# Two conditioning products moved from the second attention into the first feed-forward

## The chip, the core and the metric

The kernel runs on one core of a Trainium2 chip. A core has five engines that run their own instruction streams and meet at semaphores: TensorE (PE, with its weight loads shown as PEld), VectorE (DVE), ScalarE (ACT), GpSimd (POOL) and SyncE (SP). SP issues nearly all transfers here, one after the other from one queue; the transfers themselves are carried by the core's 16 DMA engines. The metric is the device time of one execution in microseconds (us); less is better. The times below are medians over runs, and the profile is of one further execution.

## The reference

One inference step of a two-layer encoder for 1024 prompt positions and 8 x 16 sample positions (1152 tokens, width 1024). Both layers have the same frame; `c` is a conditioning vector, one for the prompt and one for each sample:

```
ada = silu(c) @ w_ada[l] + b_ada[l]        # six pieces of 1024: shift, scale, gate, twice
h   = x * (1 + sc_m) + sh_m
x   = layer_norm(ALPHA * x + (1 + g_m) * attention(h))
h   = x * (1 + sc_f) + sh_f
x   = layer_norm(ALPHA * x + (1 + g_f) * conv_ffn(h))
```

The first layer attends over its own chunk of 64 and the two before it, the second over its own and the eight before it, with keys and values that are projected once from the first layer's output under a shift and scale of their own. `conv_ffn` projects up to 2 x 2816 columns, applies a causal convolution of width 3, multiplies `gelu` of one half by the other, and projects down. Sample positions have caches of keys, values and convolution rows.

## The kernel before

Everything is in 32 bit. A product of activations and weights is made of three passes over a high and a low part of each (`mmT`, L266, and `mmX`, L278); ACT makes the high part of a weight tile and POOL or DVE the low part (`split`, L160), after SP has loaded it into one of the two staging buffers `ws` (`wload`, L164). The parts go into a ring of weight slots.

The stages follow each other: first attention, its output projection, first feed-forward, second attention, its output projection, second feed-forward.

**The conditioning products.** The conditioning is 7 x 2048 columns, in seven products that `ada(gi, bank, ring)` computes: 0, 1 and 2 are the first layer's, 3 is that of the shared keys and values, 4, 5 and 6 are the second layer's. One product takes 16 loads of 512 KB of `in_adaw` (L207) and two float32 matmuls for each (L210) into one PSUM bank, with only 32 columns of `c` as the stationary side. Then it loads its bias four times (L197), adds it (L222), for products 1, 2, 5 and 6 adds 1 to the gate's part on POOL (L229) and writes that to `gd` in DRAM (L230), and brings the rest into `adaT` by four transposes (L235) and a copy (L237). A product is a generator: it yields after each load with its two matmuls, and after each part of its end, 18 steps in all.

Products run in the background of other work: `self.bg` holds a list of them, and `step(n)` adds `n` to a sum and runs one step of the list for each whole 1 in it. In the feed-forward `wload` calls it once for each weight tile, with `self.bgrate`; in the attention the loop over pairs calls it once a pair with `BGA` (0.6). `drain()` runs what is left. The buffers of a product are those of its ring: without one, the two `ws` buffers; in the first feed-forward `fr`, three buffers of `F` (`hf`, `xr`, `tmp`) that lie idle there until its last group.

**The attention** (`attention(l)`) first projects keys and values and writes them to DRAM (`kH` with a high and a low part, `vH` with both). Its loop then runs over 16 heads with four pairs of query blocks each. A head's keys are loaded by `kload` (L433), once a head for the high part and once for the low part, into buffers of which there is one set for even and one for odd heads:

```
for t, k in ((khi[a], kh), (klo[a], kl)):
    nc.sync.dma_start(t.bitcast(F32), bass.AP(k.tensor, k.offset, [[0, 2], [1024, 64], [1, 1024]]))
```

For each pair PE makes scores (L504, L507), DVE and ACT the softmax (L470, L474), PE transposes the weights (L530) and multiplies them by the values (L549). Query projections (L266, weights through `ws`) and 16 sample items with loads of their caches (L597 to L605; products at L615 and L650) are spread through the loop. Scores rotate over four PSUM banks; the products of the background use a bank of their own, bank 4, and once the list is empty scores rotate over five.

**The feed-forward** (`ffn(l)`) goes through 22 tile columns in groups of two: up-projections (L266), convolution on ACT and DVE (L978, L981), and the down-projection of the group before (L1052). The order in which each engine gets its instructions is made by a scheduler from the program, before the kernel runs; on the chip every engine keeps to it.

Of the kernel before, what the change touches and what calls it, by code (L numbers as in the profile page):

```python
# [32 lines left out]
UP = ({0: (0, 1), 2: (2,)}, {0: (0, 1), 3: (2,)})  # L33
LV = (0, 1, 2, 8, 3, 4, 5, 6, 7)
BGA = 0.6
BGF = 0.8
QAT = {}
for c in range(5):
    QAT[8 * c] = [(c + 1, None)]
# [48 lines left out]
class Trunk:  # L88
# [1090 lines left out]
    def build(self):  # L1179
        nc, I, O = self.nc, self.I, self.O  # L1180
        self.bgrate = 0
        ct = self.F[:, 12288:12544]
        nc.sync.dma_start(ct, I["cT"])
        nc.sync.dma_start(self.lnT, I["lnT"])
        nc.scalar.activation(self.cT, ct, AF.Exp, scale=-1.0)
        nc.vector.tensor_scalar_add(self.cT, self.cT, 1.0)
        nc.vector.reciprocal(self.cT, self.cT)
        nc.vector.tensor_mul(self.cT, self.cT, ct)
        x1 = self.x1p.tile([128, 9216], F32, name="x1in", tag="x1")
        big = [self.F[:, i * 1024 : i * 1024 + 1024] for i in range(10)]  # L1190
        big = Ring(big + [x1[:, i * 1024 : i * 1024 + 1024] for i in range(3, 9)])
        xs = [t.rearrange("p (c t) -> p c t", t=384) for t in (x1[:, 0:3072], self.F[:, 0:3072], self.F[:, 3072:6144])]
        for _ in self.ada(0, 0, big, self.F[:, 10240:11264]):
            pass
        wk = [self.wload(I["wk0"][0], el="v")]
        nc.sync.dma_start(xs[0], I["xT"][0])
        wk.append(self.wload(I["wk0"][1]))
        self.first_h(self.affine(0, (0, 1), e="v"), xs)
        self.bg = [self.ada(1, 4), self.ada(2, 4)]
        self.tables()  # L1200
        self.attention(0, wk)
        self.drain()
        aff = self.affine(0, (3, 4), 0)
        self.out_proj(0, I["xrow"], self.xd[0], aff)
        fr = Ring([self.hf, self.xr, self.tmp])
        self.bg = [self.ada(g, 7, fr) for g in (3, 4)]
        self.bgrate = BGF
        self.ffn(0, self.xd[0], self.zd, lambda: self.affine(3, (6, 7), 1))
        self.bgrate = 0
        self.bg = [self.ada(5, 4), self.ada(6, 4)]  # L1210
        self.attention(1, None)
        self.drain()
        self.out_proj(1, self.xd[1], self.xd[2], self.affine(5, (11, 12), 2))
        self.ffn(1, self.xd[2], O["y"], lambda: None)
# [130 lines left out]
```

## Time and profile before

| | |
|---|---|
| median of 3 runs | 3365.52 us (3361.0 to 3370.13) |
| profiled execution: its own time | 3361.58 us |
| profiled execution: span, first to last instruction | 3359.7 us |
| mean granted TensorE clock | 0.931 |
| PE busy | 2928.3 us, 87% |
| DVE, ACT, POOL busy | 46%, 34%, 27% |
| `ws<-in_adaw_dram` loads | 64 of 512 KB |
| `F<-in_adaw_dram` loads | 42 of 512 KB |

In the rows of the profile "out<-in" names the buffers that an instruction writes and reads, "L210" is a line of the kernel, "x256" the number of instructions. A float32 matmul of the program appears as two records, so that one product has 64 records of L210. Idle time before a group is followed by what ended it ("<-DMA ws<-in_adaw_dram"). SPq is SP's queue: the time there is from an issue's start to its end. Records of a `busy` column can overlap, so that mean times the number can be more than busy time. The rows by stage give for each engine busy us and, in brackets, the number of instructions.

### The profile page before, as it was taken

To read this page: it belongs to the slowest core of one execution; us is meant where nothing else is said; L and a number is where in the kernel's file an instruction comes from. 1 tells how busy PE (TensorE), PEld (TensorE's weight loads), DVE (VectorE), ACT (ScalarE), POOL (GpSimd) and SP (SyncE) were. 2 spreads that over 40 slices of the span, in tenths; PEclk is the share of its full clock that TensorE was granted. 3 is DMA by queue.
4 is the path that set the end of the run, shared out by engine and by line. 5 is a ranking of instruction groups with operands and counts; after the bars stand their busy time and mean duration, and the time that the engine had idled before them with its cause. 6 is when DMAs were issued, how large, how long until landed. Compare 5 with 4: busy or idle time off the path is not lost. (4 is left out here: it accounts for less than half of the span.)

```text
span 3359.7 us, 42671 instructions
## 1 busy us (share of the span) xinstructions
PE 2928.3 (87%) x16524; PEld 2591.7 (77%) x16524; DVE 1549.9 (46%) x3162; ACT 1132.1 (34%) x2400; POOL 922.7 (27%) x745
## 2 busy tenths in 40 slices
PE   7796967899999999998886676666789999999996
PEld 5684755788988899978885555465679999999995
DVE  4253556524444444592123344344582444444458
ACT  3263522432222222243244344343244222222224
POOL 3021212422222222444511111120253223222243
PEclk8898888999999999999998888787889999999998
DMA  7334385622222211136754334447731111111121
GB/s 284 125 126 142 123 184 124 218 70 69 67 69 72 67 50 38 63 130 214 265 180 131 117 113 149 140 131 195 162 125 50 45 44 39 46 45 38 38 70 77
DMA packets 216283, 372.78 MB, mean 111 GB/s; under 512 B 34168, under 2 KB 138424, under 8 KB 215696
## 3 DMA queue, kind: packets, MB, share of 16 engines
q1 hardware_dynamic: 205808, 336.49, 32.5%
q0 software_dynamic: 10272, 33.56, 2.8%
q8 instruction: 130, 2.13, 0.3%
q14 instruction: 73, 0.60, 0.1%
HBM read 294.65 MB, written 84.79 MB: 113 GB/s over the span
## 5 line engine op out<-in xcount | busy, mean ns | idle before, releaser
L266 PE MATMUL PS<-H,wh 128*128 128x384 f32 (+1 forms) x5472 | 1057.5, 340 | 0.3 <-DVE H L160 0.3
L266 PEld LDWEIGHTS PS<-H,wh 128*128 128x128 f32 x5472 | 975.2, 189 | 12.6 <-issue 2.5
L266 PE MATMUL PS<-H,wl 128*128 128x384 f32 (+1 forms) x2736 | 569.4, 346 | 55.3 <-DVE X L327 22.5
L160 POOL TENSOR_TENSOR wl<-ws,wh 128x1024 fp32r<-128x1024 f32 x167 | 405.5, 2435 | 769.5 <-ACT wh L149 748.2
L981 DVE SCALAR_TENSOR_TENSOR F<-PS,F 128x256 f32<-128x256 f32 (+2 forms) x704 | 352.5, 512 | 485.1 <-ACT F L978 474.0
L266 PEld LDWEIGHTS PS<-H,wl 128*128 128x128 f32 x2736 | 492.9, 192 | 89.3 <-issue 53.3
L1052 PE MATMUL PS<-wh,X 128*128 128x512 f32 x1584 | 468.4, 395 | 18.5 <-DVE X L160 9.3
L978 ACT ACTIVATE F<-PS,F 128x384 f32<-128x384 f32 x264 | 177.3, 672 | 682.5 <-PE PS L266 674.2
L1052 PEld LDWEIGHTS PS<-wh,X 128*128 128x128 f32 x1584 | 294.8, 188 | 79.1 <-DVE X L160 11.0
L1043 DVE TENSOR_TENSOR acc<-acc,PS 128x512 f32<-128x512 f32 x324 | 221.3, 685 | 267.5 <-PE PS L1052 266.9
L1027 POOL TENSOR_TENSOR F<-F 128x384 f32<-128x384 f32 x132 | 138.9, 1052 | 634.5 <-ACT F L1025 632.2
L1052 PE MATMUL PS<-wl,X 128*128 128x512 f32 x792 | 246.7, 392 | 0.0
L278 PE MATMUL PS<-wh,H 128*128 128x256 f32 (+1 forms) x1008 | 197.5, 324 | 44.6 <-DVE H L160 31.8
L149 ACT CAST wh<-ws 128x1024 fp32r<-128x1024 f32 x176 | 181.6, 1043 | 155.7 <-PE PS L1052 88.4
L278 PEld LDWEIGHTS PS<-wh,H 128*128 128x128 f32 x1008 | 152.6, 196 | 59.8 <-DVE H L160 33.0
L160 DVE TENSOR_TENSOR X<-F,X 128x384 fp32r<-128x384 f32 x132 | 153.0, 1159 | 97.8 <-ACT X L149 95.8
L564 POOL DMA_DIRECT2D oT<-F x96 | 52.4, 546 | 480.4 <-ACT F L561 339.7
L1052 PEld LDWEIGHTS PS<-wl,X 128*128 128x128 f32 x792 | 149.4, 189 | 33.9
L210 PE MATMUL PS<-ws,C 128*32 128x512 f32 x256 | 74.3, 709 | 109.4 <-DMA ws<-in_adaw_dram 109.4
L470 DVE CUSTOM_DVE_ANT_0 F<-PS,F,C 128x256 f32<-128x256 f32 (+3 forms) x208 | 97.2, 480 | 122.3 <-PE PS L507 89.1
L470 DVE CUSTOM_DVE_ANT_0 F<-PS,F 128x320 f32<-128x320 f32 (+5 forms) x144 | 67.5, 481 | 162.2 <-PE PS L530 73.2
L530 PE MATMUL PS<-C,F 128*128 128x128 f32 x720 | 127.7, 294 | 2.3 <-DVE wl L536 0.7
(199 smaller groups left out, 3329.2 us busy)
## 6 DMA issues: line engine op xcount, KB each, us to landing
ws<-in_wup_dram SPq DMA_DIRECT2D x88, 512.0 KB
ws<-in_adaw_dram SPq DMA_DIRECT2D x64, 512.0 KB
ws<-in_wdn_dram SPq DMA_DIRECT2D x44, 512.0 KB
F<-in_adaw_dram SPq DMA_DIRECT2D x42, 512.0 KB
X<-oT SPq DMA_DIRECT2D x64, 256.0 KB
x1att<-kH SPq DMA_DIRECT2D x30, 512.0 KB
F<-xd SPq DMA_DIRECT2D x27, 512.0 KB
vH<-X SPq DMA_DIRECT2D x40, 256.0 KB
```

Source lines behind the costliest of these rows:

```text
L149: nc.scalar.copy(out, in_)
L160: self.eng(el).tensor_sub(lo, src, hi.bitcast(F32))
L210: nc.tensor.matmul(ps[32 * j : 32 * j + 32, :], self.cT[:, k * 32 : k * 32 + 32], w[:, j2 * 512 : j2 * 512 + 512], start=k == 0, stop=k == ...
L266: self.nc.tensor.matmul(out[:, 0:n], w[a][:, k * 128 : k * 128 + 128], H[:, p, k, s0 : s0 + n], start=i == 0, stop=i == 23)
L278: self.nc.tensor.matmul(out[:, 0:n], H[:, p, j * kn + k, t0 : t0 + 128], w[a][:, k * n : k * n + n], start=i == 0, stop=i == 23,)
L470: nc.vector.tensor_tensor_reduce(out=p[:, c0 : c0 + w], in0=ps, in1=b, scale=1.0, scalar=init, op0=ALU.add, op1=ALU.min, accum_out=nm)
L530: nc.tensor.transpose(t[:, m * 128 : m * 128 + 128], p[:, (kt - k0) * 128 : (kt - k0) * 128 + 128], self.ident)
L978: nc.scalar.activation(y, ps[:, off : off + 384], AF.Identity, bias=w(3), scale=w(2))
L981: nc.vector.scalar_tensor_tensor(o, u, w(i), o, op0=ALU.mult, op1=ALU.add)
L1027: nc.gpsimd.tensor_mul(a, y, ya[bi])
L1043: nc.vector.tensor_add(row[:, n], row[:, n], ps)
L1052: nc.tensor.matmul(ps, ac[m][p][:, cs], w[m][q][:, n], start=i == 0, stop=i == 5)
```

## The change

The list of the first feed-forward gets all four products 3 to 6, through the same three buffers and bank 7, and the rate of its steps per weight tile is raised from 0.8 to 1.25. The second attention starts with an empty list.

```
-BGF = 0.8
+BGF = 1.25
...
         fr = Ring([self.hf, self.xr, self.tmp])
-        self.bg = [self.ada(g, 7, fr) for g in (3, 4)]
+        self.bg = [self.ada(g, 7, fr) for g in (3, 4, 5, 6)]
         self.bgrate = BGF
         self.ffn(0, self.xd[0], self.zd, lambda: self.affine(3, (6, 7), 1))
         self.bgrate = 0
-        self.bg = [self.ada(5, 4), self.ada(6, 4)]
         self.attention(1, None)
```

The condition under which scores rotate over five banks (`if not self.bg`) holds from the first pair on.

More of the change, by code (lines that the diff above doesn't have):

```diff
@@ L35 @@
 BGA = 0.6
-BGF = 0.8
+BGF = 1.25
 QAT = {}
@@ L1205, in build @@
         fr = Ring([self.hf, self.xr, self.tmp])
-        self.bg = [self.ada(g, 7, fr) for g in (3, 4)]
+        self.bg = [self.ada(g, 7, fr) for g in (3, 4, 5, 6)]
         self.bgrate = BGF
@@ L1209, in build @@
         self.bgrate = 0
-        self.bg = [self.ada(5, 4), self.ada(6, 4)]
         self.attention(1, None)
```

## The prediction

> **What bounds the kernel now.** I read the page first, then busy time by stage, then the groups of each stage with what ended their waits, then SP's own queue. From the page:
>
> ```profile
> span 3359.7 us, 42671 instructions
> PE 2928.3 (87%) x16524; PEld 2591.7 (77%) x16524; DVE 1549.9 (46%) x3162; ACT 1132.1 (34%) x2400; POOL 922.7 (27%) x745
> ...
> PE 31%; DMA 10%; DVE 3%; SPq 1%; POOL 1%; issue 1%; ACT 1%; POOLq 0%; DVEq 0%; ACTq 0%
> PE PS L266 18%; PE PS L1052 7%; DMA ws<-in_adaw_dram 3%; DMA x1att<-kH 2%; PE PS L549 1%; DMA F<-in_cvB_dram 1%; PE PS L530 1%; PE PS L210 1%; DMA wl<-kH 1%; PE PS L504 1%; DMA X<-oT 1%; PE PS L507 1%; PE PS L278 1%; SPq L921 1%; DMA F<-xd 1%
> ```
>
> PE is the bound in most of the span. The one large transfer in the chain is the load of the conditioning weights (`in_adaw`) into `ws`, the two staging buffers that the attention's own weights use too. Busy time by stage, in the order PE, PEld, DVE, ACT, POOL, then granted clock, DMA share and GB/s:
>
> ```profile
> 690.00:1100.00 410.00, 410.00 (x2110) 364.16 (x2110) 167.93 (x272) 112.70 (x190) 111.00 (x86) 1.00 0.22 72
> 1770.00:2160.00 390.00, 259.98 (x1710) 211.35 (x1709) 146.97 (x453) 152.48 (x384) 52.59 (x86) 0.82 0.41 128
> 2160.00:2313.00 153.00, 101.20 (x828) 83.24 (x826) 70.47 (x235) 66.11 (x171) 23.05 (x35) 0.83 0.47 145
> ```
>
> The first row is the first feed-forward: PE busy without a gap. The others are the loop over pairs of the second attention, with conditioning products in it (to 2160) and after them: PE is idle a third of both, and no other engine is half busy. So in the stage that receives the work each PE microsecond is paid whole; the stage that gives it up waits for transfers. Its groups, with idle time before them and its cause last:
>
> ```profile
> L210 PE MATMUL PS<-ws,C 128*32 128x512 f32 x112 | 33.8, 745 | 94.8 <-DMA ws<-in_adaw_dram 94.8
> ...
> L650 PE MATMUL PS<-F 128*32 128x128 f32 (+1 forms) x384 | 21.5, 327 | 24.6 <-DMA F<-in_cvB_dram 22.9 <-ACT F L474 1.1 <-issue 0.6
> ```
>
> The loop's longest PE wait is for conditioning weights (94.8 us); a sample item's cache (L650) and the head's keys (`kH`, below) follow.
>
> **Why those loads are late.** The key loads (L433) and who waited for them; rows of SP's queue in order of time; two rows of PE's; and the DMA engines from 1907 to 1922 us in 40 slices (tenths busy, then GB/s):
>
> ```profile
> L433 SPq DMA_DIRECT2D x1att<-kH x21: 484/512/1358, 1784.0 to 2245.6; - x21
> L433 SPq DMA_DIRECT2D wl<-kH x7: 484/491/2770, 1826.9 to 2246.2; - x7
> ...
>   PE PS L507: 37.7, 5
> ```
>
> ```profile
> 1926.28 1.11 SPq L433 DMA_DIRECT2D x1att<-kH  x2
> ...
> 1960.43 0.51 SPq L433 DMA_DIRECT2D x1att<-kH  x1
> ...
> 1967.76 3.31 SPq L207 DMA_DIRECT2D ws<-in_adaw_dram  x2
> ...
> 2148.12 1.99 SPq L433 DMA_DIRECT2D x1att<-kH  x2
> ...
> 2189.62 0.53 SPq L433 DMA_DIRECT2D x1att<-kH  x1
> ...
> 2221.18 1.11 SPq L433 DMA_DIRECT2D x1att<-kH  x2
> ```
>
> ```profile
> 1954.01 0.48 PE L507 MATMUL PS<-x1att 128*128 128x128 f32 x1 [7.46 <-DMA x1att<-kH]
> ...
> 1987.92 1.92 PE L210 MATMUL PS<-ws,C 128*32 128x512 f32 x4 [16.09 <-DMA ws<-in_adaw_dram]
> ```
>
> ```profile
> DMA  1314799821111111111111111111111111100000
> GB/s 44 93 66 109 208 393 371 339 66 66 44 44 66 44 66 44 44 66 44 66 44 44 66 44 66 44 55 55 44 66 44 49 60 44 60 38 22 33 11 0
> ```
>
> A key pair issued at 1926.28 released PE at 1954.01: 27.7 us. A conditioning load issued at 1967.76, behind the pair of 1960.43, was there at 1987.92: 20.2 us. Between short bursts near 370 GB/s the engines are one to two tenths busy at about 50 GB/s. A key load takes its 64 rows twice, with the 2 as the outermost step (L433); two 512 KB loads at 50 GB/s are 21 us, most of the 27.7. What is issued behind them waits for them. At 370 GB/s a conditioning load itself needs 1.4 us.
>
> The Trainium skill, DMA: Bandwidth & Descriptors, Rules for kernel authors, says that an outermost dimension of c below 16, such as a leading broadcast of c copies, confines a transfer to at most c engines. The trace agrees: two of sixteen engines would be 0.125, and the slices show a tenth.
>
> **The change part by part.** *Added to the first feed-forward:* products 5 and 6, each 16 loads of 512 KB, 32 matmuls (64 records), 4 bias loads, one DVE add, two POOL adds, two small `gd` writes, 4 transposes and a DVE copy. PE's price there, for the two products already in that stage, and how SP stood in it:
>
> ```profile
> L266 PE MATMUL PS<-H,wl 128*128 128x386 f32 (+1 forms) x880 | 179.6, 341 | 0.0
> ...
> L210 PE MATMUL PS<-F,C 128*32 128x512 f32 x104 | 23.2, 605 | 0.0
> L235 PE MATMUL PS<-C,F 128*128 128x128 f32 x8 | 1.2, 272 | 0.0
> ```
>
> ```profile
> 1096.17 35.05 SPq L207 DMA_DIRECT2D F<-in_adaw_dram  x2
> ```
>
> ```profile
> L230 SPq DMA_DIRECT2D gd<-ws x4: 995/5364/9467, 1896.4 to 2163.9; - x4
> ```
>
> 104 records are 26 loads: 0.89 us per load. 32 more loads cost 28.5 us, the transposes 1.2 us (8 records, as in the row): **+29.7 us**, between 17 us (if all loads ran in pairs of column groups, two in about 1.07 us) and 34 us (each alone, 1.05 us). DVE (168 of 410 us) and POOL (111 of 410) take their adds without being late. SP: with 0.8 raised to 1.25 steps per weight load, the three buffers turn over faster and SP is held more often at a load whose buffer is still read; behind it stand the feed-forward's weights. The row of 1096.17 shows such a hold of 35 us, and PE waited 0.0 us for weights. In the built order of the changed kernel the weight loads stand at the same places against PE as before, some 40 us of PE work ahead of their use; I take nothing. The `gd` writes stand in SP's queue until POOL has added: the same 40 us cover them. Without that cover each pair would cost what SP stood there in the attention, up to 9.5 us (the row of L230, ns: least, median, most).
>
> 61 weight loads lie before the drain; at 1.25 steps 58 of them carry the 72 steps of four products, so none is left over. The two buffers that the residual rows want next come free later than before, but still one group ahead of their use: nothing.
>
> *Taken from the second attention:* the same two products. L210 over the stage, from a window that starts before the loop (1730 to 2340):
>
> ```profile
> sum 610.00, PE 38.06 PEld 4.75; mean PE 1.90 PEld 0.24
> ```
>
> 38.1 us of PE and 94.8 us of waits: 132.9 us at most, if nothing else is late. That I don't take, since the key loads come next. While one head's four pairs run, the next pair of key loads must land, and buffers allow no more than one head ahead. The loop issues 14 pairs (21 and 7 loads, the first at 1784.0); the eleventh is that of 2148.12, so ten heads took 364.1 us. PE without conditioning has only about 20 us per head there (259.98 less 33.8, over some 11.5 heads: the eleventh pair is issued when the eleventh head's scores are done), so without conditioning the key loads set the pace. For six heads without sample items I take the pair's 27.7 us, for four with items 31.6 us (2189.62 to 2221.18, the first gap behind the last product's tail): 6 x 27.7 + 4 x 31.6 = 292.6, **71.5 us less**. The heads after 2148 are as they are. Before 1784 about 5 us of L210's work and waits go. Together **-76 us**; the ends are -133 (above) and -42 (the second rival).
>
> By the 27 GiB/s per engine that the Trainium skill gives (DMA: Bandwidth & Descriptors, Specifications), a pair on two engines would take an estimated 18 us instead of 21, ten heads would win 30 us more, and the sum below would be 3286 us; the slices' 50 GB/s are what this case measures, and the sum goes by them.
>
> *Also moved:* with no products left, scores turn over five banks from the first pair, not four. PE's waits for the softmax in the loop are below 3 us in all: nothing either way. The clock granted in the loop is 0.82; a rise would shorten PE's 20 us per head, which the loads cover: nothing.
>
> **Sum.** -76 + 30 = -46 us on the profiled execution's 3361.6 us: 3316 us. The median of the runs is 3365.5, 0.12% above that execution; on it the sum is 3319.
>
> **The rivals.**
> *The waits simply go.* Keys and caches arrive as they do now and the full 132.9 us is won: 3361.6 - 132.9 + 29.7 = 3258 us. For it: these waits lie on PE, in the chain. Against it: 27.7 us landing against 20 us of PE work per head.
>
> *The two slow engines are the bound.* If they are never free in the loop, all that goes is the time conditioning loads spend on them: 32 x 1.4 = 45 us at 370 GB/s, 42 at 400; I take 42. 3361.6 - 42 + 29.7 = 3349 us. For it: the 50 GB/s slices, and SP holding. Against: fourteen heads' pairs at 21 us are 294 of 543 us; with 5 us a head for other traffic and 45 for conditioning the engines are about four fifths used. The skill's rule named above is what would make this so.
>
> *Slower: PE waits for conditioning weights in the feed-forward.* The changed order has about nine places where three loads' products stand together; the next product follows some 8.5 us after the first of them and needs the buffer that first one frees. A transfer that took 17 us, as behind key loads, would hold PE 8.5 us at each: 77 us, and 3361.6 - 76 + 30 + 77 = 3392 us. It decides from 5 us at each place. For it: PE has no gap to hide it. Against it: no two-engine load runs there, DMA is at 0.22, and a load lands in about 3 us when nothing is ahead of it:
>
> ```profile
> 3245.25 3.12 DMA ws<-in_wdn_dram
> ```
>
> **How the numbers follow.** Forecast 0.66, waits simply go 0.10, two slow engines 0.11, slower 0.13. Measurements here tell about 0.3% (10 us) from no change. The forecast and the first rival are faster; of the second (-12 us) I count 0.05 as faster and 0.06 as no change; the third is slower, and 0.01 of the forecast's tail is no change. So faster 0.80, same 0.07, slower 0.13. The range runs from 3268 (between forecast and full gain) to 3362 (no gain): it leaves the slower case and part of the first rival outside.
>
> **What would show it.** In the changed profile L210 reads only `F` after the first attention; in the first feed-forward it has 256 records of which all but a few loads wait 0, and the stage is about 30 us longer with PE still full. In the second attention's loop the `in_adaw` wait is gone, and L507's wait for `kH` has grown from 38 us to some 80; key pairs are issued every 28 us early and every 31 later. If key waits stay near 38 us the first rival holds; if key pairs still come every 35 us the second; if L210 shows waits for `F<-in_adaw` of 45 us or more, the third. The prediction is wrong above all if SP's order, not the two engines, sets when key pairs are issued.

## The result, and the profile after

The changed kernel takes 3324.46 us (median of 4 runs, 3322.9 to 3328.68), the kernel before beside it 3367.82 us: a ratio of 0.9875, 95% interval 0.9855 to 0.9895, or 43 us less. The forecast was 46 us less. The profiled execution took 3324.77 us. Its page:

```profile
span 3322.8 us, 42663 instructions
...
PE 2927.7 (88%) x16524; PEld 2598.2 (78%) x16524; DVE 1553.0 (47%) x3162; ACT 1130.4 (34%) x2400; POOL 920.5 (28%) x745
...
PE 29%; DMA 10%; DVE 2%; SPq 1%; issue 1%; POOL 1%; ACT 1%; POOLq 0%; DVEq 0%; ACTq 0%
PE PS L266 18%; PE PS L1052 7%; DMA x1att<-kH 4%; DMA ws<-in_wo_dram 1%; DMA F<-in_cvB_dram 1%; PE PS L530 1%; PE PS L549 1%; DMA X<-oT 1%; DMA wl<-kH 1%; PE PS L504 1%; SPq L921 1%; PE PS L507 1%; DMA F<-xd 1%; PE PS L650 0%; POOL wl L160 0%
```

The load of conditioning weights is gone from the chain. The DMA share of the chain is still a tenth: the key loads have doubled to 4%, and the weights of the output projection (`in_wo`) are new.

Two landmarks bound the first feed-forward: its first down-projection (L1052) and the first transpose of its closing norm (L849 on `acc`). Before, then after; behind the colon least, median and most ns, then first and last start:

```profile
L1052 PEld LDWEIGHTS PS<-wh,X x1584: 186/188/333, 651.1 to 3339.9; 128*128 128x128 f32 x198
...
L849 PEld LDWEIGHTS PS<-C,acc x72: 138/141/230, 1473.1 to 1536.3; 128*128 128x128 f32 x72
```

```profile
L1052 PEld LDWEIGHTS PS<-wh,X x1584: 186/188/333, 651.9 to 3303.3; 128*128 128x128 f32 x198
...
L849 PEld LDWEIGHTS PS<-C,acc x72: 138/141/232, 1503.8 to 1568.3; 128*128 128x128 f32 x72
```

822.0 us became 851.9: 29.9 us more. The groups of this stage after the change, and the stretch that stood in the prediction:

```profile
L210 PE MATMUL PS<-F,C 128*32 128x512 f32 x252 | 53.8, 604 | 0.0
L235 PE MATMUL PS<-C,F 128*128 128x128 f32 x16 | 2.4, 272 | 0.0
```

```profile
690.00:1100.00 410.00, 410.00 (x2110) 357.49 (x2109) 164.93 (x265) 112.27 (x188) 109.64 (x88) 1.00 0.25 83
```

252 records for 53.8 us are 0.85 us per load, none of them waited for, and PE is full as before. The other side of the balance is the second attention's loop. Its key loads:

```profile
L433 SPq DMA_DIRECT2D x1att<-kH x21: 484/522/10615, 1816.9 to 2213.1; - x21
...
L433 SPq DMA_DIRECT2D wl<-kH x7: 485/2243/10622, 1840.7 to 2213.6; - x7
```

```profile
1816.88 13.22 SPq L433 DMA_DIRECT2D x1att<-kH  x3
...
2101.06 1.07 SPq L433 DMA_DIRECT2D x1att<-kH  x2
...
2213.05 0.51 SPq L433 DMA_DIRECT2D x1att<-kH  x1
```

The first key pair is issued at 1816.88, the eleventh at 2101.06, the last at 2213.05. So the ten heads that took 364.1 us take 284.2, 79.9 less; the three after them take 112.0 instead of 97.5, 14.5 more. What PE waits for in the loop now:

```profile
L530 PE MATMUL PS<-C,F 128*128 128x128 f32 x480 | 84.1, 297 | 37.1 <-DVE X L536 21.8 <-DVE wh L536 14.5 <-DVE wl L536 0.3
...
L507 PE MATMUL PS<-x1att 128*128 128x320 f32 (+4 forms) x84 | 31.0, 371 | 51.2 <-DMA x1att<-kH 51.2
...
L507 PE MATMUL PS<-wl,x1att 128*128 128x320 f32 (+3 forms) x84 | 27.4, 329 | 10.2 <-DMA wl<-kH 10.2
...
L650 PE MATMUL PS<-F 128*32 128x128 f32 (+1 forms) x384 | 19.4, 316 | 34.5 <-DMA F<-in_cvB_dram 32.8 <-ACT F L474 1.1 <-issue 0.6
```

The 94.8 us for conditioning weights are gone; the waits for keys rose from 37.7 to 61.4 us, those for a sample item's values from 22.9 to 32.8, and 37 us of waits behind DVE's L536 are new. Where the largest of these comes from is seen on SP (two rows), ACT, DVE and PE:

```profile
2173.30 1.14 SPq L433 DMA_DIRECT2D x1att<-kH  x2
2176.95 8.15 SPq L164 DMA_DIRECT2D ws<-in_wo_dram  x1
```

```profile
2201.64 1.04 ACT L149 CAST x1att<-ws 128x1024 fp32r<-128x1024 f32 x1 [21.05 <-DMA ws<-in_wo_dram]
```

```profile
2203.20 1.02 DVE L536 TENSOR_TENSOR X<-PS,X 128x512 fp32r<-128x512 f32 x2 [21.90 <-ACT X L535]
```

```profile
2203.95 1.54 PE L530 MATMUL PS<-C,F 128*128 128x128 f32 x6 [21.76 <-DVE X L536]
```

A load of `wo` for the output projection, whose issue starts 3.6 us behind that of a key pair, is there 24.7 us later; for 8.15 us of these SP itself stands in the issue. ACT has its cast in order ahead of the softmax's copies and stands 21 us; DVE's subtraction waits for ACT, PE's next transposes for DVE. The waits were not only removed: the queue behind the key loads found other work to hold.

### The profile page after: what moved, and what is told of

Same layout as the page of the kernel before. It is cut to its first block, busy times and chain, and to the rows that moved or that the text cites. A ratio compares the mean times of both kernels' runs of the same rounds, so it can differ in the third digit from the quotient of the medians.

```text
span 3322.8 us, 42663 instructions
## 1 busy us (share of the span) xinstructions
PE 2927.7 (88%) x16524; PEld 2598.2 (78%) x16524; DVE 1553.0 (47%) x3162; ACT 1130.4 (34%) x2400; POOL 920.5 (28%) x745
## 3 DMA queue, kind: packets, MB, share of 16 engines
q1 hardware_dynamic: 205808, 336.49, 32.6%
## 5 line engine op out<-in xcount | busy, mean ns | idle before, releaser
L1052 PE MATMUL PS<-wh,X 128*128 128x512 f32 x1584 | 470.7, 396 | 18.4 <-DVE X L160 9.0
L1052 PEld LDWEIGHTS PS<-wh,X 128*128 128x128 f32 x1584 | 294.9, 189 | 82.1 <-DVE X L160 11.0
L1052 PE MATMUL PS<-wl,X 128*128 128x512 f32 x792 | 247.1, 393 | 0.0
L1052 PEld LDWEIGHTS PS<-wl,X 128*128 128x128 f32 x792 | 149.4, 189 | 33.6
L530 PEld LDWEIGHTS PS<-C,F 128*128 128x128 f32 x720 | 90.5, 150 | 54.5 <-DVE X L536 24.0
```

What stands on the lines that cost most here:

```text
L530: nc.tensor.transpose(t[:, m * 128 : m * 128 + 128], p[:, (kt - k0) * 128 : (kt - k0) * 128 + 128], self.ident)
L1052: nc.tensor.matmul(ps, ac[m][p][:, cs], w[m][q][:, n], start=i == 0, stop=i == 5)
```

## The experiments

All ratios are against the kernel before, measured beside each run; its median was 3367 to 3369 us each time.

**The form of the key loads.** The same bytes to the same places, in the second attention, but as two loads whose outermost step is the 64 rows:

```
             for t, k in ((khi[a], kh), (klo[a], kl)):
-                nc.sync.dma_start(t.bitcast(F32), bass.AP(k.tensor, k.offset, [[0, 2], [1024, 64], [1, 1024]]))
+                if l == 0:
+                    nc.sync.dma_start(t.bitcast(F32), bass.AP(k.tensor, k.offset, [[0, 2], [1024, 64], [1, 1024]]))
+                else:
+                    for r in (0, 64):
+                        nc.sync.dma_start(t[r : r + 64].bitcast(F32), k)
```

In the changed kernel:

> The changed kernel, with each key load of the second attention as two loads of 64 rows (64 outermost on both sides) instead of one whose outermost step is the 2 of the broadcast. Same bytes, 28 more issues on SP. If a key load is slow because it runs on two engines: no more stretches at 50 GB/s in the loop, PE's wait for keys (61 us there) falls below 10 us, the wait behind the output projection's weights (22 us) and most of the caches' 33 us go with it; the loop loses 80 to 100 us, time 3225 to 3250 us. If keys are late for the sum of all traffic or for SP's order: within 10 us of 3324 us.

Measured: 3153.15 us (3148.8 to 3155.58), 0.9361 of the kernel before (0.9347 to 0.9375), 171 us below the changed kernel. Its loop, from the first scores to the last, by stage as above, and the groups of the keys in it (L511 is the line that was L507):

```profile
1767.00:2092.00 325.00, 311.52 (x2420) 280.25 (x2419) 213.36 (x678) 214.52 (x550) 67.91 (x112) 0.97 0.62 173
```

```profile
L511 PE MATMUL PS<-wl,x1att 128*128 128x320 f32 (+4 forms) x84 | 26.7, 322 | 0.0
L511 PE MATMUL PS<-x1att 128*128 128x320 f32 (+4 forms) x84 | 26.3, 315 | 0.0
...
L654 PE MATMUL PS<-F 128*32 128x128 f32 (+1 forms) x336 | 15.2, 289 | 6.2 <-DMA F<-in_cvB_dram 6.1
```

325 us instead of 479, PE busy 96% of it and its clock at 0.97 instead of 0.77 to 0.85, no wait for keys at all. The engines from 1840 to 1855 in 40 slices, as in the prediction, with key loads under way:

```profile
DMA  8999999999899999999963110002600080000000
GB/s 168 179 177 232 279 292 305 341 206 195 309 388 244 227 311 281 229 363 358 358 254 145 66 44 22 0 0 87 262 0 0 0 350 0 0 22 0 0 0 0
```

Eight or nine tenths busy and then all but empty, where the unsplit form showed one or two tenths for some 10 of 15 us. So the form of the key load held the loop.

The trace also lists every DMA packet with its start and its time. In the kernel before, from 1911 to 1920 us (the low stretch of the slices in the prediction), two packets of 4 KB are in flight for 8.6 of 9 us; each takes 159 ns, which is 26 GB/s for one and 52 for two. In the changed kernel's loop exactly two packets are in flight for 216 of 479 us, in the split kernel's for 6 of 325. This fits two engines with one packet each.

A second thing goes with the form: in the unsplit kernels SP itself stands in its issues. Of the 124 issues in the changed kernel's loop 27 take more than 3 us each, 218 us together; of the 152 in the split kernel's none does. Its key loads, to be compared with the rows of L433 above:

```profile
L437 SPq DMA_DIRECT2D x1att<-kH x42: 444/560/611, 1788.7 to 2048.3; - x42
...
L437 SPq DMA_DIRECT2D wl<-kH x14: 541/588/1259, 1803.0 to 2051.0; - x14
```

I had expected the loop to lose 80 to 100 us and the time to be 3225 to 3250 us. The loop lost 154 us: 126 us of PE's idle time (139 to 13) and 28 us of its busy time (339.6 to 311.5) at the higher clock. Another 27 us went between the first feed-forward and the first scores (at 1793.7, then 1766.7 us), and 10 us were lost behind the loop. In the kernel before:

> The kernel before, with the same split of the key loads, products 5 and 6 still behind the second attention. If the conditioning loads were late because they stood behind key loads on two engines: PE's wait for them falls from 95 us to below 25 us, time 3235 to 3270 us, and the move is then worth 5 to 25 us only (PE's own price is 38 us there and 30 us in the feed-forward). Rival, that they were late because the two staging buffers let only one load run ahead: the wait stays at 60 us or more, and this kernel is 60 us or more behind the changed one with the same split.

Measured: 3145.57 us (3142.51 to 3149.54), 0.9341 (0.9327 to 0.9355). Conditioning products 5 and 6 are still in its loop:

```profile
L210 PE MATMUL PS<-ws,C 128*32 128x512 f32 x128 | 31.4, 633 | 5.5 <-DMA ws<-in_adaw_dram 5.5
```

PE waits 5.5 us for them instead of 94.8, with the same two staging buffers and the same place. So the conditioning loads were late because of the key loads ahead of them, not because of the buffers. The time is some 90 us below the 3235 to 3270 us that I had expected, as with the changed kernel. And the move is not worth 5 to 25 us there, as I had written: the moved kernel is 7.6 us slower, 0.24%, about what a measurement can tell. The prices have become equal. The loop with products 5 and 6 takes 354 us, 29 us more than the 325 without them; in the first feed-forward they cost 30.

```profile
1734.00:2088.00 354.00, 339.93 (x2538) 283.18 (x2539) 216.31 (x679) 216.39 (x548) 75.15 (x120) 0.98 0.72 207
```

**The split in both attentions.** The first attention uses the same `kload`; here the split has no `if`.

```
-                nc.sync.dma_start(t.bitcast(F32), bass.AP(k.tensor, k.offset, [[0, 2], [1024, 64], [1, 1024]]))
+                for r in (0, 64):
+                    nc.sync.dma_start(t[r : r + 64].bitcast(F32), k)
```

In the kernel before:

> The kernel before with the key loads split in both attentions. In the first attention four heads' worth of keys is loaded, PE waits 18 us for them and 11 us for conditioning weights. If those loads too are slow by their form: 15 to 35 us less than with the second attention's split alone, 3110 to 3130 us. Rival, that the first attention has other work under these waits: within 10 us of 3146 us.

3088.87 us (3087.57 to 3092.23), 0.9169 (0.9155 to 0.9183): 57 us less than with the second attention's split alone, more than the 15 to 35 of my count. I had counted PE's waits for keys and for conditioning weights (18 and 11 us) and overlooked a third one ahead of the first scores: the writes of the values (`vH<-X`) stand among the key loads on SP, ACT waits for the buffers that they free, DVE for ACT, and PE for DVE's L327. With the second attention's split alone:

```profile
L266 PE MATMUL PS<-H,wl 128*128 128x384 f32 (+1 forms) x312 | 71.7, 367 | 34.0 <-DVE X L327 23.0 <-DVE H L151 7.8 <-POOL wl L160 1.7
```

With both split that wait is 1.3 us instead of 23.0, and PE waits for no keys in the first attention. In the changed kernel:

> The changed kernel with key loads split in both attentions, nothing else. It parts the two edits of the paired kernel (3061 us). The first attention's split took 57 us from the kernel before: 3153 less 57 is 3096 us, 7 us above the kernel before with the same split (3089 us), so that the move is again a small loss; the pairing is then worth 35 us, more than the 20 us that I had for it. If pairing is worth just the 26 us that L210's group shows (53.8 to 28.4 us): 3087 us.

3087.24 us (3085.13 to 3096.59), 0.9167 (0.9152 to 0.9183): 1.6 us from the kernel before with the same split. With keys on time the move changes nothing that can be measured. (That 3087 us is also the second count of the expectation is luck: its 26 us are a misreading, of which below.)

**The fifth score bank.** The changed kernel, and later the split and the paired one, with scores on four banks in the second attention:

```
-            if not self.bg and len(sbk.items) == 4:
+            if l == 0 and not self.bg and len(sbk.items) == 4:
```

> The changed kernel with scores on four banks through the whole second attention, so without the fifth bank that comes with the empty list. My prediction: the fifth bank is worth nothing, within 3 us of 3324 us. Rival, that part of the 67 us that the loop won is the fifth bank's: 10 to 30 us slower.

> The changed kernel with split key loads and scores on four banks throughout. With scores on four banks the unsplit kernel lost 8.6 us. If the bank itself carries that (softmax of one pair under the scores of the next), it counts at least as much where PE no longer waits for keys: 3160 to 3170 us. If it was the shifted order against late loads: within 3 us of 3153 us.

3333.09 us (3330.47 to 3335.03), 8.6 us more than the changed kernel; but with split keys 3140.22 us (3134.46 to 3146.71), 13 us less than with five. Both expectations missed, in opposite directions. The bank count changes the order in which the scheduler lays out the whole attention: PE's instructions stand in another order in the traces. (While the kernel before has products in its list, it too scores on four banks; split, it takes 3145.57 us, 5 us from the 3140.22 of the moved one on four.) In the profiled executions of the split pair (3153.2 and 3146.7 us) the loops are alike, last scores at 2091.4 and 2092.7; in the output projection behind, PE waits 12 us less for the normed rows (24.2 instead of 36.1). Which step of the order does that I did not find out.

**The rate alone.** The kernel before with

```
-BGF = 0.8
+BGF = 1.25
```

> The kernel before with the rate alone raised to 1.25, both lists as before. My prediction: the same two products come earlier in the first feed-forward at the same price, within 3 us of the kernel before. Rival, that bunched loads cost PE time of their own: 5 us or more slower.

3365.62 us (3356.84 to 3372.69), 0.9993 (0.998 to 1.0006): no difference.

**Two buffers instead of three**, in the changed kernel, for the slower rival:

```
-        fr = Ring([self.hf, self.xr, self.tmp])
+        fr = Ring([self.hf, self.xr])
```

> The changed kernel with two instead of three buffers for the conditioning loads of the first feed-forward. It asks how near the slower rival was. If a load there lands in about 3 us, two buffers still suffice for most places: PE waits below 15 us in all, within 15 us of 3324 us. If loads come late there: 30 us or more slower.

3326.32 us (3322.53 to 3327.97), 1.9 us from the changed kernel: even with a buffer less no wait arises. The rival was far away.

**The price of a load on PE.** Each of these matmuls has 32 stationary columns, and the kernel places it in one of four groups of 32 columns side by side; a load's two matmuls use two of the four. Here both loads of a row are made first, and then their four matmuls; the split is in both attentions.

```
-BGF = 1.25
+BGF = 0.7
...
         for k in range(8):
+            ws = []
             for hf in range(2):
                 w = ring.next()
                 nc.sync.dma_start(w, self.I["adaw"][gi, k, hf])
-                for j2 in range(2):
-                    j = hf * 2 + j2
+                ws.append(w)
+                if pair and hf == 0:
+                    continue
+                for j in range(4) if pair else (2 * hf, 2 * hf + 1):
+                    w, j2 = ws[j // 2], j % 2
...
-        fr = Ring([self.hf, self.xr, self.tmp])
-        self.bg = [self.ada(g, 7, fr) for g in (3, 4, 5, 6)]
+        fr = Ring([self.hf, self.xr, self.tmp, self.zt])
+        self.bg = [self.ada(g, 7, fr, pair=True) for g in (3, 4, 5, 6)]
```

> The changed kernel with key loads split in both attentions, and in the first feed-forward both halves of a conditioning row together (two loads, then four matmuls on four column groups; four buffers instead of three, rate 0.7 for half as many steps). If a load's price there is 0.85 us because its two column groups leave half of PE unused, 64 loads cost 34 us instead of 55 us: 20 us less than the changed kernel with the same split, which by the other run of this call is some 25 us below 3153 us: 3105 to 3115 us. Rival, that the price is per matmul: 3125 to 3135 us.

3060.93 us (3057.91 to 3070.39), 0.9089 (0.9071 to 0.9108), 26 us less than the changed kernel with the same split; the 3105 to 3115 us expected were too high because the first attention's split was worth 66 us there and not 25. The group over the whole feed-forward in the changed kernel with the same split, then here, and one row of its time line here (eight records are two loads):

```profile
L210 PE MATMUL PS<-F,C 128*32 128x512 f32 x256 | 54.9, 604 | 2.6 <-DMA F<-in_adaw_dram 2.6
...
L214 PE MATMUL PS<-F,C 128*32 128x512 f32 x256 | 34.5, 604 | 2.5 <-DMA F<-in_adaw_dram 2.5
```

```profile
701.75 1.06 PE L214 MATMUL PS<-F,C 128*32 128x512 f32 x8
```

1.06 us for two loads; in the changed kernel a load alone takes 1.05:

```profile
695.88 1.05 PE L210 MATMUL PS<-F,C 128*32 128x512 f32 x4
```

The group fell from 54.9 to 34.5 us, 20.4 us less, as the first count had it; the other 6 of the 26 us I can't place, and the runs of this kernel spread over 12. (The 53.8 and 28.4 us in an expectation above are no such pair: they count 252 records and 216, because this kernel's feed-forward starts 55 us earlier and its first loads lie ahead of 655 us, where both counts begin.) This is the fastest kernel measured, 307 us below the kernel before. The same with four score banks:

> The paired kernel with scores on four banks in the second attention. If four banks are better once keys are there: 8 to 13 us less than 3061 us. If that difference was an accident of the order: within 5 us, either way.

3063.06 us (3061.69 to 3069.57): no difference from five. And with products 5 and 6 back behind the second attention, where they stay single:

```
-BGF = 0.7
+BGF = 0.4
...
-        self.bg = [self.ada(g, 7, fr, pair=True) for g in (3, 4, 5, 6)]
+        self.bg = [self.ada(g, 7, fr, pair=True) for g in (3, 4)]
...
+        self.bg = [self.ada(5, 4), self.ada(6, 4)]
         self.attention(1, None)
```

> Split key loads and paired conditioning loads in the first feed-forward, but with products 5 and 6 behind the second attention as in the kernel before (single loads there, rate 0.4 for the two products that stay). It asks whether the move pays once its price is halved. By prices: in the feed-forward two products cost 15 us paired, in the attention 31 us of PE and 5 us of waits; so 10 to 20 us above the paired kernel, 3071 to 3081 us. If the attention hides part of that: within 5 us of 3061 us.

3073.15 us (3070.5 to 3077.95), 0.9129 (0.9115 to 0.9143). By the medians the move is worth 12.2 us again (0.4%), once its price in the feed-forward is reduced, within the 10 to 20 expected. The profiled executions, 3070.39 (the slowest of the paired kernel) and 3072.47, lie only 2 us apart, so they do not show where the 12 us are won.

## Why the prediction was right

**The price in the first feed-forward.** Forecast +29.7 us, measured +29.9 between landmarks. It was an addition of PE time to a stage where PE has no gap, and the price per load came from the same stage.

**Its covers.** The weight loads, the bias loads and the `gd` writes cost nothing there, as written: PE is busy 410.00 of 410 us, and neither a higher rate nor a buffer less changed the time. The reason given for L230's 9.5 us was wrong, though: with split key loads the same writes, behind the same adds on POOL, take 0.28 to 1.84 us of SP (the last for two). SP stood there in issues behind key loads, not for POOL.

**The ten heads.** Forecast 71.5 us less, measured 79.9. The step that named the key loads as the next bound is what kept the forecast from the full 132.9 us, and the split showed it: without the two-row form there is no wait for keys, and with it the waits for keys grew by 24 us. The details fit less well than the sum. The first six heads took 25.6 us each and not 27.7, the next four 32.6 and not 31.6; the key waits grew to 61.4 us and not to some 80; and pairs were not issued every 28 and 31 us but 12.7 to 41.4 us apart. A pair's time from issue to landing was a fair estimate of the average pace, not the pace of each head.

**The heads after them.** This step failed: "The heads after 2148 are as they are." They took 14.5 us more. The step put the loads of the output projection's weights at nothing without a reason. The scheduler puts them among the key loads, and they stand behind these like any other. Before, the first of them was issued at 2145.42, behind the last load of conditioning weights; now it is at 2007.62. Of the 37.1 us that PE waits for DVE's L536, 36.5 fall in these last heads.

**Before the first key pair.** "About 5 us" of L210's work and waits were to go. The stretch from the first scores (1760.6, then 1793.7) to the first pair is 23.4 us before and 23.2 after; nothing went there.

**The fifth bank.** "Nothing either way" was not borne out as a number: 8.6 us one way, 13 the other, 2 in a third kernel. No value of the bank itself is shown. That a changed order moves the time by about 10 us in either direction fits the three pairs, but no run holds the order fixed, so it is not shown.

**The rivals.** The waits did not simply go. That the two slow engines are the bound was right in kind and wrong in degree: they had room for more than the 42 us given to it. (Its sum was also a little off: 294 us of key pairs, 5 us for each of 14 heads and 45 for conditioning are 409 of 543 us, three quarters and not four fifths.) The profile does not name the engine of a packet; that the slow form uses two is read from the two packets in flight, and from the tenth and about 50 GB/s in the slices. The rule in the Trainium skill (DMA: Bandwidth & Descriptors, Rules for kernel authors) says the same. What the runs show is that the form is the cause. The slower rival had no part in it.

Sum: +29.9 in the feed-forward, -79.9 and +14.5 in the heads, and some -1 elsewhere give the -36.8 us between the two profiled executions; the medians lie 43 us apart. That this is so near the forecast of -46 is partly luck: the ten heads came out 8.4 us better than forecast, the heads after them 14.5 and the stretch before them 5 us worse, and these misses partly cancel. The mechanism, a price of 30 us paid whole in the feed-forward against an attention that then waits for its keys, held.

## What to carry to other kernels

When an engine waits for a transfer, look at what stands ahead of that transfer before moving it: the load that was late here cost 95 us only because slow loads were in front; with these made fast, the same load cost 5.5. A move takes the late load away and leaves the slow one to delay the next; a change in the slow load's form was worth four to five times the move, and made the move worthless until its own price in the feed-forward was cut. Slices with a tenth of the DMA engines busy at a steady low rate, while something waits, are the sign to look for.

## What was not expected

A load of 512 KB with a leading step of 2 ran at about 50 GB/s, against peaks near 370 for loads over 128 rows, and two loads followed behind it were there 20.2 and 24.7 us after their issue began. Two halves in its place, with 28 more issues in the loop, took 171 and 223 us off the two kernels in the second attention, and a further 57 to 66 in the first, where 23 us of waits behind the value writes went with those for keys. With PE's share in the loop risen from 71% (339.58 of 479 us) to 96% its granted clock rose from about 0.8 to 0.97, and the same work without conditioning took 311.5 us of PE instead of 339.6.

```profile
sum 479.00, PE 339.58 PEld 303.24 DVE 214.40 ACT 216.03 POOL 67.67; mean PE 169.79 PEld 151.62 DVE 107.20 ACT 108.02 POOL 33.83
```
